# Two layers of a hybrid trunk: the first up phase by seven products of halves, the modulation sums in small steps across four stages

## The chip, the cores and the metric

The kernel runs on 1 core of a Trainium2 chip. The metric is device time in microseconds (us) of one execution. The core has TensorE (PE; its weight loads are shown as PEld), VectorE (DVE), ScalarE (ACT), GpSimd (POOL), and SyncE (SP), which here only issues DMAs from its queue, in order.

## The reference

1152 tokens (128 context, 1024 latent) of width 1024 go through two layers. Layer 0 has attention beside a short convolution, layer 1 a bidirectional recurrence with 8 heads (HGRN2); each is followed by a gated feed-forward block with a convolution. Everything is fp32.

```
def _modulation(cond, w_mod, b_mod):
    return jnp.split(jax.nn.silu(cond) @ w_mod + b_mod, 6, axis=-1)

def _conv_ffn(h, w_up, conv_w, w_down):
    u = _dwconv(h @ w_up, conv_w)          # w_up: 1024 x 5632, three taps along the tokens
    a, gt = jnp.split(u, 2, axis=-1)
    return (jax.nn.silu(gt) * a) @ w_down  # w_down: 2816 x 1024

...
    sh1_s, sc1_s, gt1_s, sh2_s, sc2_s, gt2_s = _modulation(cond_lat, w_mod[l], b_mod[l])
    xs = _layer_norm(ALPHA * xs + gt1_s * os_, ln1_g[l], ln1_b[l])
    fs = _conv_ffn(xs * (1 + sc2_s) + sh2_s, ffn_w_up[l], ffn_conv_w[l], ffn_w_down[l])
    xs = _layer_norm(ALPHA * xs + gt2_s * fs, ln2_g[l], ln2_b[l])
```

The modulation is a product of two condition vectors (context and latent) with a 1024 x 6144 matrix per layer. It is made in chunks of 512 columns, 12 per layer.

## The kernel before, in words

Every large fp32 product is made of three passes over rounded parts: `wsplit` (L103) cuts a weight into a high part (ScalarE, L108) and a low part (GpSimd, L109, or VectorE), the activations are kept as such a pair too, and `mm3` (L92) issues high x high, high x low and low x high. Its lines 93 to 95 stand for all such matmuls in the profile, so groups go by tiles. Weights come over a ring of two raw tiles and three split ones. From the end of attention on, the order of instructions on each engine is the order in which the program writes them (`manual_schedule`), and SP's DMAs keep that order too.

**Up phase of layer 0** (`ffn_up`, L941): 44 products (22 pairs of a gate and a value column block), each 3 x 8 x 3 = 72 matmuls of 388 columns into a PSUM tile of three banks ("psu"). `conv` (L969) follows one product behind, on ScalarE (L978) and VectorE (L979, 980, 984); the result goes to DRAM ("sd"). Beside it the phase makes 13 chunks of the modulation (`mod_pieces`, L154): 512 KB loads into two tiles, 16 VectorE operations (L170 for the first of each condition, L172), then eight 128 x 128 transposes on TensorE (L181) and two reductions on VectorE (L183). GpSimd makes the residual x*g + b of the nine token blocks (L265), which are stored. The first raw and split pieces of the down phase are made before the last products end.

**Up phase of layer 1** (`ffn_up_fast`, L1071): six direct products (n = 0 to 5), and meanwhile `sums` (L1125) makes differences of the halves of h on VectorE. Then 19 pairs go by seven products of halves: `operand` (L1203) makes the weight operand four products ahead (sums on VectorE, L1197 to 1201; high part on ScalarE, L1219; low part on GpSimd, L1220), `product` (L1230) issues 24 matmuls of 290 columns three-fold into a PSUM tile of two banks out of a ring of four ("psq"), and VectorE adds it into "u" (L1302 to 1313; L1313 is the last of a pair). The convolution of a pair is done during the next pair (L1243, L1248). At the seam into the seven products, line 1179 first splits the held third of the sums after the last convolution, then four operands are made (L1254). In the last pair the first two pieces of the down phase are loaded at the fifth product and split at the seventh (`split_s`, L1334), and the last modulation gate is stored at the fourth (`gate_store`, L193: 2 x 1024 pieces of 4 bytes).

**Down phase** (`ffn_down`, L1347): six groups of weight rows; in each, two column halves of nine token blocks. A unit (one half of one block) is 12 matmuls of 512 columns (6 in the first group) into one of six PSUM tiles ("psd"), copied by ScalarE in the first group (L1424) and added by VectorE in the others (L1426). In layer 1 alone the affine rows are loaded and scaled first (L1396, 1397, "gb"), and the residual is made unit by unit from the stored blocks (`residual_of`, L1400), with loads and stores over SP. The fifth group also multiplies by the gate on GpSimd (L1449) and adds on VectorE (L1453).

**Heads** (L1950 to 2033): for each of 8 heads 21 level steps (L1960) with projections for the next head between them.

Of the kernel before, what the change touches and what calls it, by code (L numbers as in the profile page):

```python
# [80 lines left out]
def build(tc, ins, outs, consts):  # L81
# [72 lines left out]
    def mod_pieces(l, f0, psp, tag):  # L154
# [30 lines left out]
        return load, compute, finish  # L185

# [754 lines left out]
    def ffn_up(l, hT, mod_list, xdst, steps, y, dw):  # L941

        with ExitStack() as st:
            fp = st.enter_context(tc.tile_pool(name=f"fp{l}", reuse_waits="tile", bufs=1))
            nonlocal accp, mbufs
            accp, mbufs = fp, 2
            pd = st.enter_context(tc.tile_pool(name=f"pdF{l}", reuse_waits="tile", bufs=2, space=PSUM))
            pu = st.enter_context(tc.tile_pool(name=f"puF{l}", reuse_waits="tile", bufs=2, space=PSUM))
            N = 2 * NF
            ws = {0: wpre.pop(0), 1: wpre.pop(0)}  # L950
            raws = {2: wraw(*up_cols(l, 2))}
            pss, cvs, pieces = {}, {}, []

            def bank():
                return pd.tile([P, 512], F32, tag="d", name="psl")

            def tmp():
                return fp.tile([P, 768], F32, tag="ht", bufs=2, name="ht")

            def products(n, order):  # L960
                if n not in pss:
                    pss[n] = pu.tile([P, 3, 512], F32, tag="u", name="psu")
                w, ps = ws[n], pss[n]
                for c, k in order:
                    a = c * OW
                    mm3(ps[:, c, :IW], (w[0][:, k, :], w[1][:, k, :]),
                        (hT[0].k(k, a, IW), hT[1].k(k, a, IW)), k == 0, k == KT - 1)

            def conv(n):  # L969
                ps, f = pss.pop(n), n // 2 if n % 2 else NF + n // 2  # L970
                t = fp.tile([P, SW], F32, tag="cv", bufs=4, name="cv")
                t3 = t.rearrange("p (a b) -> p a b", b=OW)
                cw = [fcw[:, l * 132 + q * 44 + f:l * 132 + q * 44 + f + 1] for q in range(3)]
                if n == N - 1:
                    last = fp.tile([P, 3, IW], F32, tag="last", name="last")
                    nc.scalar.activation(last, ps[:, :, :IW], AF.Copy)
                    ps = last
                nc.scalar.activation(t3, ps[:, :, 1:1 + OW], AF.Copy, scale=cw[1])  # L978
                nc.vector.scalar_tensor_tensor(t3, ps[:, :, 0:OW], cw[0], t3, op0=ALU.mult, op1=ALU.add)  # L979
                nc.vector.scalar_tensor_tensor(t3, ps[:, :, 2:2 + OW], cw[2], t3, op0=ALU.mult, op1=ALU.add)  # L980
                if n % 2 == 0:
                    nc.scalar.activation(t, t, AF.Silu)
                else:
                    nc.vector.tensor_tensor(t, t, cvs[n - 1], op=ALU.mult)
                cvs[n] = t

            def order(c):
                return [(c, k) for k in range(KT)]

            def store(n):  # L990
                if n > 0 and n % 2:
                    nc.sync.dma_start(sd[l][n // 2], cvs.pop(n))
                    cvs.pop(n - 1)

            def prepare(n):

                if n + 3 < N:
                    raws[n + 3] = wraw(*up_cols(l, n + 3))
                elif n + 3 - N < 2:
                    raws[n + 3] = wraw(*down_unit(l, n + 3 - N))  # L1000
                if n + 2 < N:
                    ws[n + 2] = wsplit(*raws.pop(n + 2))

            def mods_ahead():
                for a in range(2):
                    if not pieces and mod_list:
                        fs = mod_pieces(*mod_list.pop(0), pd, "d")
                        pieces.extend([(fs, b) for b in range(4)])
                    if pieces:
                        fs, b = pieces.pop(0)  # L1010
                        fs[0](b)
                        ready.append((fs, b))
            ready, ends = [], []
            gb = affine_rows(fp, l, 0)
            for n in range(N):

                while ends and ends[0][0] <= n - 2:
                    ends.pop(0)[1]()
                if n == 0:

                    for c in (2, 1, 0):
                        todo = steps.get(c - 1, [])
                        for x in range(2):
                            for kh in range(2):
                                products(x, order(c)[4 * kh:4 * kh + 4])
                                if todo:
                                    todo.pop(0)(bank, tmp)
                    nc.scalar.activation(gb, gb, AF.Copy, scale=ALPHA)
                elif n > 1:

                    products(n, order(2) + order(1) + order(0) if n < N - 1 else
                             [(c, 4 * kh + k) for kh in range(2) for c in (2, 1, 0) for k in range(4)])
                ws.pop(n)
                store(n - 2)
                if n == N - 1:

                    for u in range(2):
                        dws[u] = wsplit(*raws.pop(N + u))
                if n:
                    conv(n - 1)  # L1040
                prepare(n)
                for fs, b in ready:
                    fs[1](b)
                    if b == 3:
                        ends.append((n, fs[2]))
                ready.clear()
                if 2 <= n <= 18 and n % 2 == 0:
                    t = NT - n // 2
                    residual(y[t], gb, (nc.gpsimd, nc.gpsimd))
                if 4 <= n <= 20 and n % 2 == 0:  # L1050
                    t = NT + 1 - n // 2
                    nc.sync.dma_start(rows_of(xdst, t), y[t])
                if n >= 1:
                    mods_ahead()
                if n == 32:
                    gate_store(l, 5)
                if n == N - 4:
                    for a in range(2):
                        sraws.append(sraw(l, a, dw))
                if n == N - 1:  # L1060
                    for f in range(2):
                        split_s(l, f, dw)
                if l == 0 and n == 20:
                    gate_store(1, 2)
            conv(N - 1)
            store(N - 1)
            for _, f in ends:
                f()

    sraws = []  # L1070
    def ffn_up_fast(l, hT, steps, y):  # L1071
# [31 lines left out]
        def conv(n):  # L1103
            ps = pss.pop(n)
            t = fp.tile([P, 1160], F32, tag="t", bufs=3, name="cv")[:, :SW]
# [4 lines left out]
            nc.vector.scalar_tensor_tensor(t3, ps[:, :, 2:2 + OW], cw[2], t3, op0=ALU.mult, op1=ALU.add)  # L1110
            if n % 2 == 0:
# [3 lines left out]
            cvs[n] = t  # L1115
# [25 lines left out]
        for n in range(N0):  # L1141
            if n == 0:
                for c in (2, 1, 0):
                    todo = steps.get(c - 1, [])
                    for x in range(2):
                        for kh in range(2):
                            products(x, [(c, 4 * kh + k) for k in range(4)])
                            if todo:
                                todo.pop(0)(bank, tmp)
            elif n > 1:  # L1150
                products(n, [(c, k) for c in (2, 1, 0) for k in range(KT)])
            ws.pop(n)
            if n > 2 and n % 2:
                nc.sync.dma_start(sd[l][n // 2 - 1], cvs.pop(n - 2))
            if n:
                conv(n - 1)
            if n + 3 < N0 + 2:
                raws[n + 3] = wraw(*up_cols(l, n + 3))
            if n + 2 < N0:
                ws[n + 2] = wsplit(*raws.pop(n + 2))  # L1160
# [13 lines left out]
            if 1 <= n <= 4:  # L1174
                sums(n - 1)
# [997 lines left out]
```

## Time and profile before

| | us |
|---|---|
| median of 3 runs (3332.5 to 3335.68) | 3335.12 |
| the profiled execution: its own time | 3338.62 |
| its span | 3336.7 |
| TensorE busy | 3192.3 (96%) |
| VectorE busy | 2030.9 (61%) |
| GpSimd busy | 1262.8 (38%) |
| ScalarE busy | 1228.1 (37%) |

The stages: the start and attention to some 700 us, the up phase of layer 0 to 1280, its down phase to some 1590, the heads to some 2390, the up phase of layer 1 from 2492 to 3012, its down phase to the end. A timeline row gives start, duration, engine, line, operation, tiles, and in brackets how long the engine was idle before it and what ended that. Matmuls overlap, so a matmul's cost is the distance between starts.

### The profile page before, as it was taken

The numbers are of one execution on the slowest core, as the hardware profiler recorded it, in microseconds if no ns is written. First come the engines' busy times: TensorE is split into PE (matmuls) and PEld (weight loads), VectorE is DVE, ScalarE is ACT, GpSimd is POOL, SyncE is SP. The second block draws the span as 40 slices with busy tenths as digits, with TensorE's granted clock in tenths as the row PEclk, the third lists the DMA queues.
The fourth block names the chain that finished last, engine by engine and source line by source line (L and its number), as shares of the span: only waits on it lengthen the run. The fifth ranks groups of instructions, "written<-read, shape, count | busy, mean of one in ns | idle before, by whom it ended". The sixth has DMA issues, their size and how long they took to land. (4 is left out here: it accounts for less than half of the span.)

```text
span 3336.7 us, 46779 instructions
## 1 busy us (share of the span) xinstructions
PE 3192.3 (96%) x18671; PEld 2962.3 (89%) x18671; DVE 2030.9 (61%) x2912; ACT 1228.1 (37%) x2033; POOL 1262.8 (38%) x898
## 2 busy tenths in 40 slices
PE   7999999999999999998999999999999999997997
PEld 6989887789999998886999999998778999996886
DVE  5777888449997223355355455555557677773356
ACT  4412998232221224114433444433444333333112
POOL 6821333234431122242244443333424444442565
PEclk9999999999999999999999999999999999998999
DMA  7152000225564224231311111111322222225452
GB/s 216 34 145 77 1 1 32 80 79 174 160 167 132 64 74 135 87 126 44 115 62 40 49 42 55 55 49 44 114 95 73 73 73 73 74 78 145 155 175 82
DMA packets 264041, 295.87 MB, mean 89 GB/s; under 512 B 18467, under 2 KB 198895, under 8 KB 263824
## 3 DMA queue, kind: packets, MB, share of 16 engines
q1 hardware_dynamic: 263024, 291.25, 28.3%
q8 instruction: 147, 2.41, 0.3%
q0 software_dynamic: 800, 1.63, 0.2%
q14 instruction: 70, 0.57, 0.1%
HBM read 233.12 MB, written 59.72 MB: 88 GB/s over the span
## 5 line engine op out<-in xcount | busy, mean ns | idle before, releaser
L109 POOL TENSOR_TENSOR wlo<-wraw,whi 128x1024 fp32r<-128x1024 f32 x116 | 288.0, 2486 | 702.5 <-ACT whi L108 666.7
L93 PE MATMUL psd<-whi,s 128*128 128x512 f32 x720 | 286.1, 397 | 24.3 <-ACT y L1424 14.0
L94 PE MATMUL psd<-wlo,s 128*128 128x512 f32 x720 | 285.6, 397 | 0.0
L95 PE MATMUL psd<-whi,s 128*128 128x512 f32 x720 | 285.5, 397 | 0.0
L108 ACT ACTIVATE whi<-wraw 128x1024 fp32r<-128x1024 f32 x168 | 176.4, 1052 | 271.9 <-PE psd L95 82.3
L1696 POOL TENSOR_TENSOR X<-X,tot 128x384 f32<-128x384 f32 x144 | 183.4, 1274 | 212.6 <-PE pss L1690 142.9
L1426 DVE TENSOR_TENSOR y<-y,psd 128x512 f32<-128x512 f32 x144 | 98.8, 686 | 228.8 <-PE psd L95 228.6
L172 DVE SCALAR_TENSOR_TENSOR macc<-mraw,sil,macc 128x512 f32<-128x512 f32 x280 | 228.5, 881 | 14.6 <-DMA mraw<-in_w_mod_dram 14.5
L1696 DVE TENSOR_TENSOR X<-X,tot 128x384 f32<-128x384 f32 x144 | 90.3, 627 | 168.0 <-PE pss L1690 109.7
L93 PE MATMUL psu<-h,whi 128*128 128x388 f32 (+1 forms) x504 | 175.6, 349 | 14.0 <-DVE sc L600 7.6
L93 PEld LDWEIGHTS psd<-whi,s 128*128 128x128 f32 x720 | 136.6, 190 | 57.6 <-ACT y L1424 14.9
L93 PE MATMUL psu<-ra,whi 128*128 128x388 f32 x528 | 180.9, 343 | 2.9 <-DVE y L912 2.7
L95 PE MATMUL psu<-rb,wlo 128*128 128x388 f32 x528 | 179.9, 341 | 0.0
L94 PE MATMUL psu<-rb,whi 128*128 128x388 f32 x528 | 179.7, 340 | 0.0
L94 PE MATMUL psu<-ra,whi 128*128 128x388 f32 x528 | 179.6, 340 | 0.0
L93 PE MATMUL psu<-rb,whi 128*128 128x388 f32 x528 | 179.6, 340 | 0.0
L95 PE MATMUL psu<-ra,wlo 128*128 128x388 f32 x528 | 179.4, 340 | 0.0
L94 PE MATMUL psu<-h,whi 128*128 128x388 f32 (+1 forms) x504 | 174.7, 347 | 2.5 <-POOL h L389 2.4
L93 PE MATMUL psp<-s,whi 128*128 128x384 f32 x480 | 175.1, 365 | 0.0
L1690 PE MATMUL pss<-X,km 128*128 128x128 f32 x1008 | 152.4, 288 | 22.2 <-ACT km L1679 10.3
L95 PE MATMUL psu<-h,wlo 128*128 128x388 f32 (+1 forms) x504 | 173.2, 344 | 0.0
L93 PE MATMUL psp<-h,whi 128*128 128x384 f32 x480 | 173.1, 361 | 0.0
(413 smaller groups left out, 9645.9 us busy)
## 6 DMA issues: line engine op xcount, KB each, us to landing
wraw<-in_ffn_w_up_dram SPq DMA_DIRECT2D x88, 512.0 KB, 4.9
mraw<-in_w_mod_dram SPq DMA_DIRECT2D x80, 512.0 KB, 4.0
sraw<-sd SPq DMA_DIRECT2D x44, 578.0 KB, 4.4
wraw<-in_ffn_w_down_dram SPq DMA_DIRECT2D x44, 512.0 KB, 4.7
wraw<-in_hgrn_w_in_dram SPq DMA_DIRECT2D x40, 512.0 KB, 3.9
sd<-cv SPq DMA_DIRECT2D x25, 579.0 KB, 5.5
sd<-t SPq DMA_DIRECT2D x19, 578.0 KB, 2.9
wraw<-in_attn_w_in_dram SPq DMA_DIRECT2D x18, 512.0 KB, 4.0
```

The costliest lines, as they stand in the source:

```text
L93: mm(ps, l[0], r[0], start=start, stop=False)
L94: mm(ps, l[0], r[1], start=False, stop=False)
L95: mm(ps, l[1], r[0], start=False, stop=stop)
L108: nc.scalar.activation(hi[:, :n], raw[:, :n], AF.Copy)
L109: (eng or nc.gpsimd).tensor_tensor(lo[:, :n], raw[:, :n], r32(hi[:, :n]), op=ALU.subtract)
L172: nc.vector.scalar_tensor_tensor(acc[:, cond, :], r, sil[:, cond, k:k + 1], acc[:, cond, :], op0=ALU.mult, op1=ALU.add)
L1426: nc.vector.tensor_tensor(y[t][:, cols], y[t][:, cols], ps, op=ALU.add)
L1690: mm(ps[:, q3 * P:(q3 + 1) * P], km[:, q3 * P:(q3 + 1) * P], scan_ap(X, QAB, QAF, c0, P, hh), start=True, stop=True)
L1696: eng.tensor_tensor(x, x, t4[:, :, :, 1 - half].unsqueeze(3).to_broadcast([P, 2, nb, hh]), op=ALU.mult)
```

## The change

Layer 0's up phase is made by the function that layer 1 used, now called for both. The modulation chunks are made by a generator, `mod_steps`, one step at a time: one 256 KB load per step into a single tile, two VectorE operations per step, and at the end of a chunk eight matmuls against a column of ones. 3 chunks are made in layer 0's up phase and 2 in layer 1's (a step after every fourth product), 4 in the first down phase (ten steps per group, groups two to five), 4 in the heads (after every second level step). At the seam into the seven products, the first four operands are made before the last convolution but one, and the held sums are split between the sums and the end of the last convolution. In the last pair, the first pieces of the down phase are loaded at the third product and split at the sixth and seventh; the gate store moves to the thirteenth of the 19 pairs; the second down unit's split moves behind the convolution. The residual of layer 0 is made in its down phase as in layer 1. The convolution tile ring goes from 3 to 2; the gate store (1, 2) moves from layer 0's up phase to the fifth head; two temporary tiles of the first down phase's tail become halves of one tile.

```
+    def mod_steps(chunks, pool, bank):
+        for l, f0 in chunks:
...
+            acc = pool.tile([P, 2, 512], F32, tag="macc", name="macc")
+            for k in range(KT):
+                raw = pool.tile([P, 512], F32, tag="mraw", name="mraw")
+                nc.sync.dma_start(raw, wm[:, k, f0:f0 + 512])
+                yield True
+                for cond in range(2):
+                    if k == 0:
+                        nc.vector.tensor_scalar(acc[:, cond, :], raw, sil[:, cond, k:k + 1], None, op0=ALU.mult)
+                    else:
+                        nc.vector.scalar_tensor_tensor(acc[:, cond, :], raw, sil[:, cond, k:k + 1], acc[:, cond, :],
+                                                       op0=ALU.mult, op1=ALU.add)
+            yield True
+            ps = bank()
+            for cond in range(2):
+                for f in range(4):
+                    mm(ps[:, 4 * cond + f:4 * cond + f + 1], acc[:, cond, f * P:(f + 1) * P], ones, start=True,
+                       stop=True)
+            nc.vector.tensor_tensor(mods[:, l, :, c0:c0 + 4], ps[:, 0:8].rearrange("p (c f) -> p c f", f=4),
+                                    colA[:, l * 48 + c0:l * 48 + c0 + 4].unsqueeze(1).to_broadcast([P, 2, 4]),
+                                    op=ALU.add)
...
-    def ffn_up(l, hT, mod_list, xdst, steps, y, dw):
...
-    def ffn_up_fast(l, hT, steps, y):
+    def ffn_up(l, hT, mod_list, steps, y):
...
+            if n == N0 - 1:
+                pr[P0] = (raws.pop(N0 + 1)[0], raws.pop(N0)[0])
+                for o in range(4):
+                    operand(o)
             if n:
                 conv(n - 1)
...
-        conv(N0 - 1)
-        first.close()
-        for j in range(4):
-            put(3, j, held[:, j, :], nc.vector)
+        conv_sums(N0 - 1)
+        for j in range(4):
+            put(3, j, held[:, j, :], nc.gpsimd if j == 1 else nc.vector)
+        conv_end(N0 - 1)
+        first.close()
...
-                if last and q == 4:
+                if last and q == 2:
                     for f in range(2):
-                        raw = tp.tile([P, 4, HW], F32, tag=f"T1{f}", name="sraw").rearrange(
+                        raw = tp.tile([P, 4, HW], F32, tag=f"T2{f}", name="sraw").rearrange(
...
-                if last and q == 6:
-                    split_s(l, 0, None)
-                    split_s(l, 1, None)
+                if last and q > 4:
+                    split_s(l, q - 5, None)
...
                     keep(p - 1, old["t1"])
-                    if last:
+                    if p == P0 + 12:
                         gate_store(l, 5)
...
+                if o % 4 == 1 and p < NP - 1:
+                    next(mod, None)
...
-        dws[1] = wsplit(*raws.pop(1))
         t2 = conv_first(NP - 1, 1, us[1])
...
         conv_rest(NP - 1, 0, us[0], t1)
+        dws[1] = wsplit(*raws.pop(1))
...
-    def ffn_down(l, xsrc, dw, tail, pre):
+    def ffn_down(l, xsrc, mod_list, dw, tail, pre):
...
-            if l:
-                gb = affine_rows(lp, l, 0)
...
+            gb = affine_rows(lp, l, 0)
+            nc.scalar.activation(gb, gb, AF.Copy, scale=ALPHA)
+            xsum = xh[1]
...
+                        if gi and ((t + hf) % 2 or t == 0):
+                            next(mod, None)
...
+    ffn_up(0, rhsA, mod_todo[:3], steps, y)
...
+    y = ffn_down(0, xd[0], mod_todo[3:7], dw, tail0, {7: lambda: (first_raw(0), first_raw(1)), 4: lambda: first_split(0),
...
+    mod = mod_steps(mod_todo[7:11], rp, pst)
...
             hd.level(*e)
+            if n % 2 and h < 7:
+                next(mod, None)
...
+        if h == 4:
+            gate_store(1, 2)
...
+    ffn_up(1, hT, mod_todo[11:], steps, y)
```

## Rows read from the trace of the kernel before

**Rows 1.** Stretches: PE, PEld, DVE, ACT, POOL busy us; PEclk, DMA share, GB/s.

```profile
800.00:900.00 100.00, 100.00 (x575) 99.90 (x574) 95.85 (x94) 20.88 (x19) 43.31 (x16) 1.00 0.56 166
1700.00:2310.00 610.00, 600.05 (x3994) 593.84 (x3993) 317.53 (x642) 242.81 (x435) 247.54 (x188) 1.00 0.16 51
2700.00:2800.00 100.00, 100.00 (x749) 100.00 (x748) 76.92 (x70) 36.27 (x49) 46.08 (x31) 1.00 0.25 81
3000.00:3100.00 100.00, 77.28 (x351) 64.21 (x351) 36.48 (x33) 33.74 (x40) 28.84 (x12) 0.88 0.50 145
```

**Rows 2.** Timeline of ScalarE, line 978, in layer 0's up phase.

```profile
784.56 1.23 ACT L978 ACTIVATE cv<-psu,fcw 128x1158 f32<-128x1158 f32 x1 [4.89 <-PE psu L95]
...
797.34 1.23 ACT L978 ACTIVATE cv<-psu,fcw 128x1158 f32<-128x1158 f32 x1 [10.61 <-PE psu L95]
...
810.97 1.23 ACT L978 ACTIVATE cv<-psu,fcw 128x1158 f32<-128x1158 f32 x1 [4.89 <-PE psu L95]
```

**Rows 3.** Stretch of layer 1's up phase, instructions of tile psq alone.

```profile
2597.60:2994.00 396.40, 396.40 (x2960) 396.40 (x2959) 92.10 (x124) 11.72 (x18) 1.00 0.22 72
```

**Rows 4.** Timeline of TensorE in attention, fp32 matmuls of 64 columns.

```profile
413.24 1.00 PE L774 MATMUL ppf<-I,osb 128*128 128x64 f32 x8
414.05 0.71 PE L656 MATMUL S<-kst,qst 128*128 128x512 f32 x2
```

**Rows 5.** TensorE in layer 1, seam into the seven products; a wait.

```profile
2572.28 0.34 PE L95 MATMUL psu<-s,wlo 128*128 128x388 f32 x1
2577.60 0.61 PE L93 MATMUL psq<-h,whi 128*128 128x290 f32 x1 [4.99 <-ACT whi L1219]
...
2594.41 0.30 PE L93 MATMUL psq<-T,whi 128*128 128x290 f32 x1
...
PE psu L93 <- DVE cv L1110: 1.7, 3, 0.7
```

**Rows 6.** Timeline of TensorE entering the down phases, layer 0, then layer 1.

```profile
1280.23 0.40 PE L93 MATMUL psd<-whi,s 128*128 128x512 f32 x1
...
3022.99 0.77 PE L93 MATMUL psd<-whi,s 128*128 128x512 f32 x1 [10.29 <-ACT t L1243]
...
3046.36 0.80 PE L93 MATMUL psd<-whi,s 128*128 128x512 f32 x1 [12.43 <-ACT y L1424]
3046.95 0.63 PE L94 MATMUL psd<-wlo,s 128*128 128x512 f32 x1
```

**Rows 7.** Same seam on ACT, DVE, SP; then DMA issues, us to landing.

```profile
3018.19 1.17 ACT L1342 ACTIVATE s<-sraw 128x1156 fp32r<-128x1156 f32 x1 [14.13 <-DMA sraw<-sd]
...
3043.91 1.91 ACT L1397 ACTIVATE gb<-gb 128x2048 f32<-128x2048 f32 x1 [15.63 <-DMA gb<-in_ln_b_dram]
...
3022.09 0.75 DVE L1313 TENSOR_TENSOR u<-u,psq 128x580 f32<-128x580 f32 x1
...
3031.37 0.32 SPq L1252 DMA_DIRECT2D sd<-t  x1
...
gd<-mods SPq DMA_DIRECT2D x2, 4.0 KB, 11.3
...
x<-xd SPq DMA_DIRECT2D x3, 512.0 KB, 6.2
...
x<-xh SPq DMA_DIRECT2D x14, 256.0 KB, 2.9
...
mraw<-in_w_mod_dram SPq DMA_DIRECT2D x80, 512.0 KB, 4.0
```

**Rows 8.** Groups by line of VectorE, 800 to 1000.

```profile
L172 DVE SCALAR_TENSOR_TENSOR macc<-mraw,sil,macc 128x512 f32<-128x512 f32 x106 | 88.2, 900 | 0.4 <-DMA mraw<-in_w_mod_dram 0.4
L170 DVE TENSOR_SCALAR macc<-mraw,sil 128x512 f32<-128x512 f32 x14 | 32.1, 2330 | 0.0
```

**Rows 9.** Stretches of layer 1's down phase, an early and the fifth group.

```profile
3122.00:3172.00 50.00, 50.00 (x217) 40.42 (x217) 19.04 (x23) 8.71 (x8) 23.86 (x10) 1.00 0.51 165
3222.00:3272.00 50.00, 49.01 (x211) 39.04 (x210) 42.65 (x39) 6.59 (x6) 44.19 (x22) 1.00 0.46 160
```

More of the change, by code (lines that the diff above doesn't have):

```diff
@@ L185, in mod_pieces @@
         return load, compute, finish
+    ones = cst.tile([P, 1], F32, name="ones")
+    nc.vector.memset(ones, 1.0)
+    def mod_steps(chunks, pool, bank):
+        for l, f0 in chunks:
+            wm = ins["w_mod"][l].rearrange("(k p) f -> p k f", p=P)
+            c0 = f0 // P
+            acc = pool.tile([P, 2, 512], F32, tag="macc", name="macc")
[18 more added lines that the diff above has]
+                                    op=ALU.add)
     pending = []
@@ L939, in down_unit @@
         return w_dn[:, f0:f0 + 2, hf * 512:(hf + 1) * 512], 2, 512
-    def ffn_up(l, hT, mod_list, xdst, steps, y, dw):
[L943 to L1068, printed above, removed]
@@ L1139, in sums @@
             put(4, j, b21, nc.gpsimd)
[L1141 to L1160, printed above, removed]
[L1161 to L1182 removed]
         P0, NP = N0 // 2, NF
         NO = 7 * (NP - P0)
[L1185 removed]
+        wts, S, pr = {}, {}, {}
         def pair_raws(p):
@@ L1252, in keep @@
             nc.sync.dma_start(sd[l][p][:, :2 * HO].rearrange("p (a b) -> p a b", b=HO), t)
-        for o in range(4):
-            operand(o)
+        for n in range(N0):
+            if n == 0:
+                for c in (2, 1, 0):
+                    todo = steps.get(c - 1, [])
+                    for x in range(2):
+                        for kh in range(2):
+                            products(x, [(c, 4 * kh + k) for k in range(4)])
+                            if todo:
+                                todo.pop(0)(bank, tmp)
+            elif n > 1:
+                products(n, [(c, k) for c in (2, 1, 0) for k in range(KT)])
+            ws.pop(n)
+            if n > 2 and n % 2:
+                nc.sync.dma_start(sd[l][n // 2 - 1], cvs.pop(n - 2))
+            if n == N0 - 1:
+                pr[P0] = (raws.pop(N0 + 1)[0], raws.pop(N0)[0])
+                for o in range(4):
+                    operand(o)
+            if n:
+                conv(n - 1)
+            if n + 3 < N0 + 2:
+                raws[n + 3] = wraw(*up_cols(l, n + 3))
+            if n + 2 < N0:
+                ws[n + 2] = wsplit(*raws.pop(n + 2))
+            if n == 0:
+                for t in range(NT - 1, -1, -1):
+                    nc.sync.dma_start(rows_of(xd[l], t), y[t])
+                ypool["st"].close()
+            if n == 1:
+                fgs.close()
+                tps = ExitStack()
+                tp = tps.enter_context(tc.tile_pool(name=f"tp{l}", reuse_waits="tile", bufs=1, side="right"))
+                for m in (1, 2, 4):
+                    ts[m] = [tp.tile([P, 4, HW], F32R, tag=f"T{m}{q}", name=f"T{m}{q}") for q in range(2)]
+                ts[3] = [hT[q].halves[0][:, :, HW:2 * HW] for q in range(2)]
+                held = tp.tile([P, 4, HW], F32, tag="u", bufs=2, name="held")
+            if 1 <= n <= 4:
+                sums(n - 1)
+        conv_sums(N0 - 1)
[3 more added lines that the diff above has]
+        first.close()
+        pq = fs.enter_context(tc.tile_pool(name=f"pq{l}", reuse_waits="tile", bufs=4, space=PSUM))
         nc.sync.dma_start(sd[l][P0 - 1], cvs.pop(N0 - 1))
         old = None
+        mod = mod_steps(mod_list, fp, lambda: pq.tile([P, 2, 512], F32, tag="q", name="psq")[:, 0, :])
         for p in range(P0, NP):
@@ L1455, in ffn_down @@
                 nc.vector.tensor_tensor(a, a, b, op=ALU.add)
+            assert next(mod, None) is None
             su.close()
@@ L1522, in build @@
     prj.close()
+    mod_todo += [(1, f0) for f0 in range(512, 6144, 512)]
+    ffn_up(0, rhsA, mod_todo[:3], steps, y)
     dwx = ExitStack()
-    dw = dwx.enter_context(tc.tile_pool(name="dw", reuse_waits="tile", bufs=1))
-    ffn_up(0, rhsA, mod_todo + [(1, f0) for f0 in range(512, 6144, 512)], xd[0], steps, y, dw)
+    dw = dwx.enter_context(tc.tile_pool(name="dw0", reuse_waits="tile", bufs=1))
     w_in = ins["hgrn_w_in"][0]
```

66 lines of the change are left out of this document (29 added, 37 removed).

## The prediction

> **What bounds the kernel now.** First the busy time by stretches [rows 1]: TensorE is busy in 100 of 100 us of both up phases and in 600 of 610 us of the heads; only around 3000 to 3100, where layer 1's up phase hands over, it falls to 77 of 100. So TensorE's instructions set the time, and the few places where it stands still. Second, what one product costs. In layer 0 ScalarE's line 978 starts once per direct product, 12.78 us apart, or 13.63 where the eight transposes of a modulation chunk lie between [rows 2]. In layer 1 the matmuls of the seven-product path run at 396.4/2960 = 0.1339 us each [rows 3]. Third, the two seams of layer 1's up phase, one into the seven products and one into the down phase, since layer 0 gets both [rows 5 to 7]. About 0.2% (6.7 us) is what a measurement of this kernel can tell from no change; the chances below go by it.
>
> **The products.** A direct pair costs 2 x 12.78 = 25.56 us; a pair by seven products is 7 x 24 = 168 matmuls x 0.1339 = 22.50 us. 19 of the 22 pairs change: 19 x 3.06 = **-58.1 us**. That layer 0 reaches layer 1's rate is taken from rows 3: same shapes, same function.
>
> **The sums' small matmuls.** Layer 0's up phase loses the transposes of 13 chunks, 13.63 - 12.78 = 0.85 us each: **-11.0**. In their place each chunk gets eight fp32 matmuls with one moving column. TensorE is the bound in all four stages that get them (3, 4, 4 and 2 chunks), so all of it counts. No such matmul is in the trace. The nearest row is line 774: four fp32 matmuls of 64 columns, eight records, 0.81 us until the next instruction starts [rows 4], so 0.20 each. The transposes (0.85/8 = 0.11 each) are the lower end, twice line 774 the upper. I take 0.20: 8 x 0.20 x 13 = **+21.1**.
> The Trainium skill ("FP8 and Floating Point Precision", TensorE Precision Notes) says that a true fp32 matmul makes four passes through the array; the eight records for four matmuls show two. By four passes of 0.1 us the term would be 42 us, not 21.
>
> **The sums' VectorE work.** Per chunk there are two first and fourteen further operations, as before. The further ones take 0.90 us on the mean of a stretch of the direct up phase, the first ones 2.33 there [rows 8]. In the up phases a step of two operations comes every four products (12.9 us) and adds some 1.8 us to a VectorE that is busy 77%, so 91%; in 800 to 900 it was at 96% and TensorE still at 100 of 100 [rows 1]. The cover is the four PSUM tiles, one product each; without it every late microsecond of VectorE would be one of TensorE. I cost it at nothing. In the heads VectorE is at 52% and TensorE is idle 10 us in 610 [rows 1]; 36 steps are added there: **+2** (0 to 15). In the down phase I take **+5** (0 to 19) for the last group, where VectorE is already busy 42.65 of 50 us [rows 9] and gets 6 steps; why a larger loss is possible there is the first rival.
>
> **The seam into the seven products.** In layer 1 the last direct matmul starts at 2572.28 and the fourth product at 2594.41 [rows 5]: 22.1 us for three products of 3.21, so 12.3 lost. It begins with the wait for the first operand (line 1219, 4.99 us). The change issues four operands one product earlier, under 12.8 us of matmuls. What is late next is the last third of the sums of h, which the third product needs 6.4 us in: the convolution's one ScalarE copy (1.2, rows 2), two VectorE passes over 1158 columns and one over 580, at most 2.0, 2.0 and 1.0 by line 172's 0.90 for 512 columns [rows 8] (an estimate). That is 6.2, just in time. I leave 1 us of stall (0 to 12.3): layer 1 **-11.3**, layer 0 **+1.0**. Layer 0's direct products now share VectorE with those sums as layer 1's do, where TensorE waits three times, 1.7 us in all [rows 5]: **+1.7**.
>
> **The seam into the down phase.** Layer 0 has none today: its first down matmul, at 1280.23, has no idle time before it. Layer 1 stands 10.29 us (from 3012.7), does six units, and stands 12.43 [rows 6]. The first stand goes back to the loads of the first pieces. They are queued behind the gate store, which takes 11.3 us to land [rows 7]; they reach ScalarE at 3018.19, and VectorE's last sum waits behind those splits until 3022.09 [rows 7]. The change moves the gate store six pairs ahead and the loads two products ahead, so they have 10 us and no store before them: that stand goes. What is late next is the second one: ScalarE waits 15.63 us for the affine rows, with the evacuations queued behind [rows 7]. Those loads are issued behind the phase's last store (3031.37) and land when some 3.8 MB have passed, which I leave as long as it is. The last store comes 9.3 us after VectorE's last sum starts (four passes and a product of the convolution lie between); that sum moves from 3022.09 to 3012.6, right after the last matmul. So all of it shifts by 9.5, and TensorE resumes at 3036.9: layer 1 **-9.5**. Layer 0 gets the same seam: 24.2 us from the last product to the resume, less six units of 1.4 (six matmuls each, 217 in 50 us in rows 9), plus 2.4 because a dozen matmuls after a stand run slower (0.63 where 0.40 is usual, rows 6; the granted clock is 0.88 in that stretch, rows 1), which costs 0.2 each: **+18.2** where it had nothing.
>
> **The rest.** The residual (18 GpSimd passes and 18 transfers) moves from layer 0's up phase to its down phase. Layer 1's down phase has it already: GpSimd is busy 23.86 of 50 us, the DMA half, and TensorE 50.00 [rows 9]; nothing. On SP each load of the sums waits until VectorE has freed the one tile, and weight loads queue behind it: in the up phases they have five products of slack, in the heads two projections; nothing. One convolution tile less means a wait on a store that has four products to land; nothing. The gate store in the heads holds up loads by its 11 us, less than those two projections; nothing.
>
> **Sum.** -58.1 - 11.0 + 21.1 + 2 + 5 - 11.3 + 1.0 + 1.7 - 9.5 + 18.2 = -40.9. The profiled execution's own time is 3338.6, so 3297.7; the median of the runs lies 3.5 below it: **3294 us**.
>
> **Rivals.** (1) *The loads of the sums in the first down phase; the slower case.* With one tile a step is a loop: landing, two operations, next issue, so about the landing plus 2.0 us. VectorE works in order, so the evacuations stand behind a late load. Ten steps come in a group of 49.9 us, 5.0 us each, 36 in all, and six PSUM tiles of 2.77 us cover 16.6 us once. Pieces of 256 KB landed in 2.9 us in the last group of layer 1, the residual's of 512 KB in 6.2 [rows 7]. At 2.9 a step fits. At 4.0 (the old 512 KB loads, rows 7) TensorE loses 36 x 1.0 - 16.6 = 19, less the 5 already counted: 3308. At 6.2 it loses 36 x 3.2 - 16.6 = 99: 3388. From a landing of 4.7 us on the change is slower than before. For it speaks that SP's order holds each load behind waits on GpSimd; against it the 2.9, the nearest row in size and stage. Chances .18 for the milder form, .06 for slower. (2) *The first pieces still come late*, because they queue behind two weight loads: both layers keep the first stand, 9.5 each: 3313; .10. (3) *The small matmuls cost twice as much*: +21, 3315; .05; the record count of line 774 speaks against it. The four passes of the Trainium skill's page named above would be this case. (4) *The affine rows land sooner*, in both layers by 5: 3284; .06. That the change doesn't do what it says is no case of its own: layer 1 already runs the path.
>
> **How the numbers follow.** Forecast .55, the others as given. Faster by over 0.2%: .91; within it .03 (landings near 4.7); slower .06. The range 3274 to 3320 holds the forecast and rivals 2, 3, 4 and the milder 1, with one seam better or worse by some 10 us.
>
> **What would show it.** Right: 100 of 100 us and some 748 matmuls per 100 us in layer 0's up phase, which ends near 1219; no wait on line 1219 at either seam; one stand of about 15 us in each layer's first down group, ended by the affine rows; VectorE waiting under 2 us a time for the sums' loads. Wrong: TensorE waiting on VectorE's line 1426 within the first down phase; a split still waiting for its load at an up phase's end; a heads' stretch longer by over 10 us.

## The result, and the profile after

The changed kernel takes 3349.78 us (median of 4 runs, 3349.18 to 3354.56), the kernel before in the same comparison 3333.81: a ratio of 1.0047, interval 1.0034 to 1.006. It is slower by 0.5%, where 3294 was forecast. The profiled execution took 3349.69 (span 3347.9), 11.1 more than that of before.

By stages, each from the first matmul into its own PSUM tile to the first into the next stage's (layer 1 to its last matmul; what lies between changes by under 1 us a time):

| stage | before | after | forecast | measured |
|---|---|---|---|---|
| layer 0 up (from 702) | 578.0 | 526.3 | -61.5 | -51.7 |
| layer 0 down, to its last group | 228.5 | 292.2 | +29.7 | **+63.7** |
| heads | 781.8 | 789.5 | +8.5 | +7.7 |
| layer 1 up and down | 828.6 | 821.5 | -17.6 | -7.1 |

So the products gave what they should, and the loss sits in the first down phase (34 us worse than forecast) and in the seams into the seven products (some 9 each). Stretches of the changed kernel, to be held against [rows 1, 9] (columns as there):

```profile
800.00:900.00 100.00, 100.00 (x748) 100.00 (x747) 84.45 (x84) 34.28 (x46) 46.60 (x30) 1.00 0.33 104
1230.00:1280.00 50.00, 34.48 (x140) 27.42 (x139) 15.68 (x12) 24.14 (x32) 12.39 (x5) 0.83 0.50 167
1280.00:1521.00 241.00, 215.36 (x893) 174.96 (x892) 149.28 (x170) 31.94 (x30) 114.00 (x51) 0.91 0.50 165
1700.00:2310.00 610.00, 598.82 (x3980) 591.13 (x3979) 357.75 (x674) 241.15 (x432) 245.77 (x186) 1.00 0.20 60
```

Up phase and heads are as full as before. The third line is the new thing: in groups two to five of the first down phase TensorE is idle for 25.6 of 241 us and at a clock of 0.91. Who it waited for, by the waits of TensorE (us in all, times, longest):

```profile
PE psd L93 <- ACT y L1337: 31.9, 2, 16.3
PE psl L210 <- DVE macc L204: 24.8, 5, 10.9
PE psq L93 <- DVE cv L1010: 15.8, 2, 7.9
```

And the same waits in TensorE's timeline, in order of time, with the small matmuls of one undisturbed chunk (916.14) ahead of them as a measure:

```profile
916.14 1.84 PE L210 MATMUL psq<-ones,macc 128*128 128x1 f32 x16
917.85 0.38 PE L93 MATMUL psq<-T,whi 128*128 128x290 f32 x1
...
795.23 0.58 PE L93 MATMUL psq<-T,whi 128*128 128x290 f32 x1 [7.87 <-DVE cv L1010]
...
1252.47 0.80 PE L93 MATMUL psd<-whi,s 128*128 128x512 f32 x1 [15.52 <-ACT y L1337]
...
1327.13 1.86 PE L210 MATMUL psl<-ones,macc 128*128 128x1 f32 x8 [5.78 <-DVE macc L204]
1329.88 1.86 PE L210 MATMUL psl<-ones,macc 128*128 128x1 f32 x8 [0.88 <-DVE macc L204]
...
1382.31 3.08 PE L210 MATMUL psl<-ones,macc 128*128 128x1 f32 x16 [4.29 <-DVE macc L204]
...
1434.96 3.54 PE L210 MATMUL psl<-ones,macc 128*128 128x1 f32 x16 [2.94 <-DVE macc L204]
...
1496.73 3.55 PE L210 MATMUL psl<-ones,macc 128*128 128x1 f32 x16 [10.88 <-DVE macc L204]
...
3058.84 0.80 PE L93 MATMUL psd<-whi,s 128*128 128x512 f32 x1 [16.34 <-ACT y L1337]
```

TensorE stands at each of the four chunk ends, since the eight matmuls that finish a chunk need VectorE's accumulators and TensorE works in order. A stand also costs what follows it: from start to start the chunk at 916.14 takes 1.71 us, those behind a stand 2.9 to 3.6. The granted clock, 1.00 (2.4 GHz) on the ten us ahead of the first and the last of these stands, is between its two levels, 2.4 and 1.2 GHz, on the mean of the ten us behind them (stretch, TensorE busy, granted clock, DMA share, GB/s):

```profile
1310.00:1320.00 10.00, 10.00 (x45) 1.00 0.68 212
1329.00:1339.00 10.00, 9.12 (x33) 0.70 0.53 184
...
1475.00:1485.00 10.00, 10.00 (x44) 1.00 0.42 144
1497.00:1507.00 10.00, 10.00 (x35) 0.56 0.61 191
```

The +63.7 is then 15.5 for the affine rows, 24.8 at the chunk ends, 13.4 for the small matmuls there (6.8 at 1.71 a chunk), and 10.0 that remains. Matmul by matmul it is the large ones: less the waits, the distances between their starts add up to 11.7 us more than before, 1.7 to 2.8 behind each of the five stands and next to nothing elsewhere (before, TensorE's waits were 1.6).

Why VectorE is late at a chunk's end, by its timeline, GpSimd's and SP's:

```profile
1301.21 5.66 DVE L204 SCALAR_TENSOR_TENSOR macc<-mraw,sil,macc 128x512 f32<-128x512 f32 x2 [4.02 <-DMA mraw<-in_w_mod_dram]
1306.79 0.67 DVE L1339 TENSOR_TENSOR y<-y,psd 128x512 f32<-128x512 f32 x1
...
1313.88 1.41 DVE L204 SCALAR_TENSOR_TENSOR macc<-mraw,sil,macc 128x512 f32<-128x512 f32 x2 [0.24 <-DMA mraw<-in_w_mod_dram]
...
1321.50 1.41 DVE L204 SCALAR_TENSOR_TENSOR macc<-mraw,sil,macc 128x512 f32<-128x512 f32 x2 [3.73 <-DMA mraw<-in_w_mod_dram]
...
1455.17 1.41 DVE L204 SCALAR_TENSOR_TENSOR macc<-mraw,sil,macc 128x512 f32<-128x512 f32 x2 [1.86 <-DMA mraw<-in_w_mod_dram]
...
1495.83 1.41 DVE L204 SCALAR_TENSOR_TENSOR macc<-mraw,sil,macc 128x512 f32<-128x512 f32 x2 [1.62 <-DMA mraw<-in_w_mod_dram]
...
1301.10 2.41 POOL L1318 TENSOR_TENSOR x<-x,gb 128x1024 f32<-128x1024 f32 x1
1303.46 2.86 POOL L109 TENSOR_TENSOR wlo<-wraw,whi 128x1024 fp32r<-128x1024 f32 x1
...
1315.32 0.33 SPq L198 DMA_DIRECT2D mraw<-in_w_mod_dram  x1
```

The loop of the one tile can be followed (SP issues the next load once VectorE has freed the tile): the pair at 1313.88 ends at 1315.29, SP issues the next load at 1315.32, VectorE waits until it is there at 1321.50. From the first to the seventh of these pairs the fourth chunk takes 40.7 us (1455.17 to 1495.83), 6.8 a step; the other three, measured alike, take 5.9, 5.5 and 5.6. A step has 5.0. Over the 24 steps counted so, the two operations take 2.2 us of the 5.9 on the mean, and 3.8 pass from their end to the next pair's start. Over 1250 to 1500 two groups of VectorE, the sums' operations and the additions of a unit (busy us, mean ns, idle before), and below them the landing of the loads (count, size, median us):

```profile
L204 DVE SCALAR_TENSOR_TENSOR macc<-mraw,sil,macc 128x512 f32<-128x512 f32 x56 | 60.1, 1114 | 52.5 <-DMA mraw<-in_w_mod_dram 52.5
L1339 DVE TENSOR_TENSOR y<-y,psd 128x512 f32<-128x512 f32 x65 | 43.8, 682 | 42.2 <-PE psd L95 42.0
```

```profile
mraw<-in_w_mod_dram SPq DMA_DIRECT2D x32, 256.0 KB, 3.0
```

The median load lands in 3.0 us, as forecast (2.9, [rows 7]), and VectorE waits 52.5 us for the loads all the same: some come late, as the one from 1315.32 to 1321.50. The seam into the seven products, on VectorE and GpSimd:

```profile
779.09 1.93 DVE L1063 TENSOR_TENSOR S<-wraw 128x512 f32<-128x512 f32 x1
...
784.49 1.78 DVE L1067 TENSOR_TENSOR S<-wraw,S 128x512 f32<-128x512 f32 x1
786.97 1.42 DVE L1009 SCALAR_TENSOR_TENSOR cv<-psu,fcw,cv 128x1158 f32<-128x1158 f32 x1 [0.69 <-ACT cv L1008]
...
792.20 1.42 DVE L1009 SCALAR_TENSOR_TENSOR cv<-psu,fcw,cv 128x1158 f32<-128x1158 f32 x1 [2.35 <-ACT cv L1008]
793.66 1.42 DVE L1010 SCALAR_TENSOR_TENSOR cv<-psu,fcw,cv 128x1158 f32<-128x1158 f32 x1
...
776.58 5.74 POOL L1030 TENSOR_TENSOR T<-b,T 128x580 fp32r<-128x580 f32 x3 [7.61 <-ACT T L1029]
```

The four weight sums of the operands (7.2 us, 1.8 each beside GpSimd's passes) run ahead of both remaining convolutions. The second of these, which frees PSUM for the second product, has its ScalarE copy (line 1008) only behind the first one's end, and ends at 795.08.

### The profile page after: what moved, and what is told of

It reads as the page before. It is cut to its first block, busy times and chain, and to the rows that moved or that the text cites. A ratio compares the mean times of both kernels' runs of the same rounds, so it can differ in the third digit from the quotient of the medians.

```text
span 3347.9 us, 48705 instructions
## 1 busy us (share of the span) xinstructions
PE 3161.8 (94%) x19231; PEld 2927.0 (87%) x19231; DVE 2230.9 (67%) x3117; ACT 1290.1 (39%) x2162; POOL 1416.1 (42%) x1007
## 5 line engine op out<-in xcount | busy, mean ns | idle before, releaser
L1086 POOL TENSOR_TENSOR wlo<-S,whi 128x512 fp32r<-128x512 f32 x152 | 243.9, 1618 | 253.9 <-ACT whi L1085 253.8
L109 POOL TENSOR_TENSOR wlo<-wraw,whi 128x1024 fp32r<-128x1024 f32 x78 | 195.6, 2510 | 248.0 <-ACT whi L108 237.1
L93 PE MATMUL psq<-T,whi 128*128 128x290 f32 x912 | 272.2, 298 | 15.8 <-DVE cv L1010 15.8
L95 PE MATMUL psq<-T,wlo 128*128 128x290 f32 x912 | 272.4, 299 | 0.0
L94 PE MATMUL psq<-T,whi 128*128 128x290 f32 x912 | 272.0, 298 | 0.0
L1114 DVE SCALAR_TENSOR_TENSOR t<-u,fcw,t 128x1156 f32<-128x1156 f32 x152 | 259.1, 1722 | 13.5 <-ACT t L1109 10.8
L108 ACT ACTIVATE whi<-wraw 128x1024 fp32r<-128x1024 f32 x130 | 136.6, 1053 | 323.6 <-DMA wraw<-in_ffn_w_down_dram 151.1
L1086 POOL TENSOR_TENSOR wlo<-wraw,whi 128x512 fp32r<-128x512 f32 x114 | 182.3, 1600 | 172.8 <-ACT whi L1085 157.1
L1085 ACT ACTIVATE whi<-S 128x512 fp32r<-128x512 f32 x152 | 93.4, 628 | 335.8 <-DVE S L1064 247.5
L204 DVE SCALAR_TENSOR_TENSOR macc<-mraw,sil,macc 128x512 f32<-128x512 f32 x182 | 185.0, 1056 | 53.8 <-DMA mraw<-in_w_mod_dram 53.8
L93 PE MATMUL psu<-h,whi 128*128 128x388 f32 (+1 forms) x504 | 176.1, 350 | 13.7 <-DVE sc L629 6.5
L93 PEld LDWEIGHTS psq<-T,whi 128*128 128x128 f32 x912 | 173.8, 191 | 16.2 <-ACT whi L1085 16.2
L1612 PE MATMUL pss<-X,km 128*128 128x128 f32 x1008 | 152.3, 288 | 23.4 <-POOL X L1618 10.4
## 6 DMA issues: line engine op xcount, KB each, us to landing
sraw<-sd SPq DMA_DIRECT2D x44, 578.0 KB, 4.6
sd<-t SPq DMA_DIRECT2D x38, 578.0 KB, 3.0
```

Of the source, the lines that this page charges most:

```text
L93: mm(ps, l[0], r[0], start=start, stop=False)
L94: mm(ps, l[0], r[1], start=False, stop=False)
L95: mm(ps, l[1], r[0], start=False, stop=stop)
L108: nc.scalar.activation(hi[:, :n], raw[:, :n], AF.Copy)
L109: (eng or nc.gpsimd).tensor_tensor(lo[:, :n], raw[:, :n], r32(hi[:, :n]), op=ALU.subtract)
L204: nc.vector.scalar_tensor_tensor(acc[:, cond, :], raw, sil[:, cond, k:k + 1], acc[:, cond, :], op0=ALU.mult, op1=ALU.add)
```

## The experiments

Each is one edit of the changed kernel (line numbers are its own, 3349.8 its median); the kernel before took 3331.7 to 3334.4 beside them.

**Without the loads of the first down phase** (e1).

```
-                raw = pool.tile([P, 512], F32, tag="mraw", name="mraw")
-                nc.sync.dma_start(raw, wm[:, k, f0:f0 + 512])
+                raw = gb[:, 0, :512]          # first down phase only
```

> The changed kernel, but the modulation sums of the first down phase read a row tile that is in SBUF already, so the 32 loads of 256 KB are left out there (those four chunks of the modulation come out as other numbers); all VectorE operations, the small matmuls and the residual stay. Theory A (the loop of one tile makes VectorE late, and TensorE, which works in order, stands at the four places where it needs a finished accumulator): TensorE's waits on line 204 in the first down phase fall from 24.8 us to under 5, the half clock behind them goes too, the stage falls from 292 to 250 to 260 us, total 3349.8 to 3310 to 3320. Rival B (GpSimd's residual passes stretch the two VectorE operations from 1.4 to 4 to 5.7 us, and that alone makes VectorE late): more than 15 us of those waits stay, total 3338 or above.

Measured: 3314.95 us. Waits of TensorE:

```profile
PE psl L213 <- DVE macc L207: 3.3, 2, 2.8
```

The same VectorE operations beside the same GpSimd passes: without the loads the stage takes 260.1 instead of 292.2. Theory A stands, as far as the loads go.

**Without the residual in layer 0's down phase**, whole (e2), its passes alone (e9), its transfers alone (e10).

```
-            stream = [... (residual_of(t, gb),) * 6]
+            stream = [... (residual_of(t, gb),) * 6] if l else []
```

> The changed kernel, but layer 0's down phase leaves the residual out (9 loads and 9 stores of 512 KB and 18 GpSimd passes; the output lacks the scale and shift of that residual); the sums and their loads stay. Theory A (loop of one tile): the waits on line 204 stay above 15 us, total 3338 to 3350. Rival B (the residual's GpSimd passes or its transfers make the sums late): the waits fall under 5 us, total 3310 to 3322.

Measured: 3325.01, waits on line 204 10.0 us in two: between the two theories, neither of which holds as written. The residual has a share in it.

```
                 for a, op in enumerate((ALU.mult, ALU.add)):
-                    nc.gpsimd.tensor_tensor(x, x, gb[:, a, :], op=op)
+                    if l: nc.gpsimd.tensor_tensor(x, x, gb[:, a, :], op=op)       # e9
+                    nc.gpsimd.tensor_tensor(x, x if l else gb[:, 1 - a, :], gb[:, a, :], op=op)  # e10, no DMAs
```

> The changed kernel, but in layer 0's down phase the residual's 18 GpSimd passes are left out; its loads and stores of 512 KB stay (the output lacks that scale and shift). e2_nores, without both, had 10.0 us of waits on line 204 and 3325. Theory P (the passes, which stretch VectorE's operations and hold the stores behind them in SP's order, are what the residual does to the sums): near e2_nores, waits 6 to 14 us, total 3321 to 3331. Theory X (its transfers, ahead of the sums' loads in SP's queue and beside them in the DMA engines): near the changed kernel, waits 20 us or more, total 3342 to 3352.

> The counterpart of e9_xfer: in layer 0's down phase the 18 GpSimd passes stay, on rows that are in SBUF, and the residual's 9 loads and 9 stores are left out (the output has the residual without scale and shift). Theory P (the passes count): near the changed kernel, waits on line 204 20 us or more, total 3342 to 3352. Theory X (the transfers count): near e2_nores, waits 6 to 14 us, total 3321 to 3331.

Measured: 3329.25 without the passes, 3347.40 without the transfers. TensorE's wait and VectorE's group (1250 to 1500), e9 first:

```profile
PE psl L210 <- DVE macc L204: 12.8, 2, 11.5
```

```profile
L204 DVE SCALAR_TENSOR_TENSOR macc<-mraw,sil,macc 128x512 f32<-128x512 f32 x56 | 48.2, 902 | 44.2 <-DMA mraw<-in_w_mod_dram 44.2
```

And e10:

```profile
PE psl L210 <- DVE macc L204: 23.4, 5, 10.2
```

```profile
L204 DVE SCALAR_TENSOR_TENSOR macc<-mraw,sil,macc 128x512 f32<-128x512 f32 x56 | 66.8, 1233 | 41.0 <-DMA mraw<-in_w_mod_dram 41.0
```

Theory P: of the residual it is the passes. Beside them one operation takes 1.1 or 1.2 us in place of 0.90, and a step has two; its 9 MB of transfers do 2 to 4 us.

**Three tiles for the loads** (e13). Two of them lie in a weight buffer that the phase needs only for its unit 20; loads go out two steps ahead.

```
-                raw = pool.tile([P, 512], F32, tag="mraw", name="mraw")
-                nc.sync.dma_start(raw, wm[:, k, f0:f0 + 512])
+                load(k + 2)                   # into tile k % 3, load(0) and load(1) ahead
                 yield True
```

> The changed kernel with three tiles for the sums' pieces in the first down phase and each load issued two steps ahead (two of the tiles lie in the third weight buffer of that phase, whose units are dealt over five buffers); all loads, operations, places and passes stay. Theory A (the one tile is the cause: each load waits for VectorE to free it, and lands too late): TensorE's waits on line 204 fall from 24.8 us to under 6, near the 3.3 of e1_noload, total 3349.8 to 3314 to 3325. Rival S (the loads are late whatever the number of tiles, since SP issues them in order behind other waits, or VectorE is simply too slow beside GpSimd): 12 us or more stay, total 3332 or above.

Measured: 3319.38. Waits of TensorE:

```profile
PE psl L218 <- DVE macc L212: 3.6, 2, 2.8
```

VectorE no longer waits for these loads at all (52.5 us before; 1250 to 1500):

```profile
L212 DVE SCALAR_TENSOR_TENSOR macc<-mraw,sil,macc 128x512 f32<-128x512 f32 x56 | 75.0, 1377 | 0.0
```

All loads, passes and operations are there, and the operations are even longer than in the changed kernel (1377 ns for 1114), so it is the one tile, at this spacing, that turns late loads and long operations into stands of TensorE. The edit also deals the phase's weights over other buffers, which was not tried by itself.

**Places of the steps.** At every second unit (e11), and the small matmuls of a chunk one step later (e6).

```
-                        if gi and ((t + hf) % 2 or t == 0):
+                        if gi and (9 * hf + 8 - t) % 2 == 0:
```

> The changed kernel with the 36 steps of the first down phase at every second unit (5.5 us apart) where they stood 2.8 or 5.5 us apart; nothing is left out. Theory D (what piles up is the neighbouring steps, two per group, which leave 2.8 us for a loop of 5 or more): waits on line 204 at 10 us or less, total 3325 to 3335. Theory M (the mean spacing of 5 to 5.5 us is itself about as long as the loop): waits 15 us or more, total 3338 to 3350.

Measured: 3344.59, waits 22.2 us in four. Theory M: 5.5 us is itself too short.

```
-            ps = bank() ... mm(...) ... nc.vector.tensor_tensor(mods...)
+            late = finish                      # called before the next chunk's first operation
```

> The changed kernel with the eight small matmuls of each chunk one step later in the order (just before the next chunk's first operation on the same accumulators), in all stages; loads, VectorE operations and their places stay. Theory (what costs is that TensorE, in order, meets the finishing matmuls at a moment when VectorE is behind): the waits on line 204 lose some 5 us at each of the four places, 24.8 to 10 or less, total 3349.8 to 3325 to 3335. Rival (VectorE's lag itself sets TensorE's pace through the six PSUM tiles): what is gained there comes back as waits of TensorE on line 1339, total 3345 to 3352.

Measured: 3337.55. The chunk ends in TensorE's timeline:

```profile
1328.39 1.05 PE L200 MATMUL psl<-ones,macc 128*128 128x1 f32 x8 [1.47 <-DVE macc L223]
...
1376.43 1.95 PE L200 MATMUL psl<-ones,macc 128*128 128x1 f32 x16 [0.76 <-DVE macc L223]
...
1424.30 1.84 PE L200 MATMUL psl<-ones,macc 128*128 128x1 f32 x16
...
1482.27 3.54 PE L200 MATMUL psl<-ones,macc 128*128 128x1 f32 x16 [17.05 <-DVE macc L223]
```

The first three stands shrink to 1.47, 0.76 and nothing, and the small matmuls behind them are faster, but the last grows from 10.88 to 17.05: lag that is not waited for stays. Neither text had that. The first down phase is 13.7 us shorter, 5.4 of it in TensorE's waits, 4.6 in the small matmuls and 3.7 in the large ones behind the stands.

**Two chunks to the heads** (e5), the steps of the other two every third unit.

```
-    y = ffn_down(0, xd[0], mod_todo[3:7], dw, tail0, ...
+    y = ffn_down(0, xd[0], mod_todo[3:5], dw, tail0, ...
-    mod = mod_steps(mod_todo[7:11], rp, pst)
+    mod = mod_steps(mod_todo[5:11], rp, pst)
-                        if gi and ((t + hf) % 2 or t == 0):
+                        if gi and (9 * hf + t + 1) % 3 == 0:
```

> The changed kernel with two of the four chunks of the first down phase moved to the heads (six there), so that 18 steps stand every third unit (8.3 us apart) where 36 stood 2.8 to 5.5 us apart; nothing is left out. Theory (a step needs some 5 to 8 us for its one tile to be freed, loaded and used, so steps closer than that pile up until a chunk's end): TensorE's waits on line 204 fall from 24.8 us to under 4 in the first down phase and stay near 0 in the heads; the down phase loses 35 to 40 us, the heads gain two chunks of 1.7 us and little else, total 3349.8 to 3312 to 3320. Rival (VectorE is too slow there with GpSimd beside it, whatever the spacing): two chunk ends are left with 5 us or more each, total 3330 or above.

Measured: 3312.75. The down phase falls to 247.9, with no wait on line 204 left; the heads grow by 9.3 for two chunks, where the first four cost 7.7 and the expectation had 3.4.

**The affine rows scaled behind the first group** (e3), and the first group's splits in its second half as well (e7).

```
-            nc.scalar.activation(gb, gb, AF.Copy, scale=ALPHA)
...
             for gi, grp in enumerate(FGROUPS[:-1]):
+                if gi == 1:
+                    nc.scalar.activation(gb, gb, AF.Copy, scale=ALPHA)
...
-                        if t in (7, 5, 4, 2) and nf < ... and (t > 3 or gi == 0):
+                        if t in (7, 5, 4, 2) and nf < ... and (t > 3 or gi == 0) and (gi or hf):   # e7
```

> The changed kernel, but ScalarE scales the affine rows behind the evacuations of the first group instead of before them, in both down phases. Theory: the two stands of TensorE (15.5 and 16.3 us, on ScalarE's line 1337) go, with some 2 us of half clock behind each; total 3349.8 to 3310 to 3320. Rival: the stand passes to the next thing that is late (the splits of the first weights, or the first residual), and less than 12 us of the 32 comes back: 3338 or above.

Measured: 3338.03. What ScalarE waits for then, and TensorE's stand:

```profile
1244.90 1.17 ACT L1256 ACTIVATE s<-sraw 128x1156 fp32r<-128x1156 f32 x1 [10.75 <-DMA sraw<-sd]
...
1246.61 0.79 PE L93 MATMUL psd<-whi,s 128*128 128x512 f32 x1 [7.68 <-ACT y L1338]
```

The rival: half of the stand passes to the next late load in ScalarE's order. At the chunk ends TensorE now waits 28.7 us where it had waited 24.8.

> As e3_gblate (affine rows scaled behind the first group), and the four splits of the first group moved from its first half to its second, so that no evacuation of the first half stands behind a load. Theory (in e3_gblate the stand is set by the load of the first split piece, which SP issues behind the phase's last store): the two stands of 7.7 and 8.7 us shrink to under 4 each, total 3338.0 to 3325 to 3332. Rival (the second group needs those four splits, so the stand only moves to its start): as e3_gblate, 3335 to 3341.

Measured: 3328.17. No wait on line 1338 is left, only some 3 us in layer 0 and 4 in layer 1 on the splits.

**Convolutions between the operands** (e4) at the seam into the seven products.

```
-                for o in range(4):
-                    operand(o)
-            if n:
-                conv(n - 1)
+                operand(0); conv_sums(n - 1); operand(1)
+                conv_sums(n); conv_end(n - 1); operand(2); operand(3)
```

> The changed kernel, but at the last direct product of both up phases the two remaining convolutions are put between the weight sums (operand 0, first convolution, operand 1, second convolution, operands 2 and 3) instead of behind all four operands. Theory: TensorE's wait for the second product (7.9 us in each layer, on line 1010) falls to 4 us or less in each, total 3349.8 to 3340 to 3344. Rival: the operands 2 and 3 then come as much later as the convolutions came earlier, the stand moves to the third or fourth product, total 3347 to 3352.

Measured: 3341.53. In layer 0:

```profile
787.77 0.38 PE L93 MATMUL psq<-T,whi 128*128 128x290 f32 x1 [3.33 <-DVE cv L1010]
...
794.01 0.40 PE L94 MATMUL psq<-ra,whi 128*128 128x290 f32 x1 [2.24 <-POOL ra L1030]
...
781.46 0.68 DVE L1063 TENSOR_TENSOR S<-wraw 128x512 f32<-128x512 f32 x1
```

The theory, with a small new wait at the third product, the one that the forecast had feared. The weight sums, which here find GpSimd idle (780.21 to 783.67), take 0.68 us each. From the first product to the fourth 6.1 us are still lost in layer 0 and 6.3 in layer 1, so the order of the convolutions explains some 8 of the 20 us lost in both; the rest was not taken apart.

**Together.** e8: e4, e5 and e7.

> The changed kernel with e4_seam, e5_heads and e7_defer together; nothing is left out. Theory: the gains add, as they lie in different places: 8 from e4_seam, 32 to 37 from e5_heads, 12 to 22 from e3_gblate and e7_defer: 3349.8 to 3283 to 3298, faster than the kernel before by 36 to 51. Rival (a stand that goes at one seam comes back behind it): 3305 or above.

Measured: 3280.21, ratio to the kernel before 0.9836 (0.982 to 0.9852): 69.6 below the changed kernel, where the three alone sum to 8.3 + 37.0 + 21.6 = 66.9. The first down phase:

```profile
1223.00:1458.00 235.00, 231.34 (x1005) 186.70 (x1005) 158.00 (x147) 57.58 (x62) 127.89 (x55) 0.99 0.56 186
```

Three variants of it: one chunk to the heads instead of two (e12); all four in the down phase through three tiles (e14); the same with the steps at every second unit (e15).

> As e8_all, but only one chunk goes to the heads: three stay in the first down phase, with steps 5.5 and 8.3 us apart by turns (6.9 on the mean); nothing is left out. If a step needs under 7 us on the mean the third chunk costs its 1.7 us in the down phase and takes some 4.6 us from the heads (what each of the two cost there, 9.2 us together): 3280.2 to 3275 to 3279. If it needs more, the waits on line 204 come back with 3 us or more: 3281 to 3292.

Measured: 3293.56, with 9.3 us of waits on line 204: 6.9 us a step is still too little for one tile, a little more costly than the expectation allowed.

> As e8_all, but with all four chunks in the first down phase, fed through three tiles as in e13_tiles, and four in the heads as in the changed kernel; nothing is left out. By theory A the two chunks cost 1.7 us each in the down phase, and the heads get back what they cost there (9.2 us in e5_heads): 3280.2 to 3272 to 3280. By rival S the waits come back: 3290 or above.

Measured: 3285.09, between the two. The heads get their 7.5 back (789.0), but the down phase takes 248.2 where e8 has 235.0. Of the 13.2 us, the small matmuls are 4.4, the waits 3.9, and the large matmuls behind the stands 4.9 (granted clock 0.83 from 1395 to 1405 and 0.70 from 1452 to 1462).

> As e14_alltiles, with the 36 steps at every second unit. If neighbouring steps still matter with three tiles: 2 to 6 us less than e14_alltiles. If not: within 2 us of it.

Measured: 3288.20, 3.1 us more than e14, which neither text had. The first down phase itself takes 248.6 where e14 has 248.2, so with three tiles the even spacing gains nothing there.

## Why the prediction was wrong

**Right.** The products: 2903 matmuls in 388.0 us, 0.1337 each as in [rows 3]:

```profile
812.00:1200.00 388.00, 388.00 (x2903) 388.00 (x2903) 88.69 (x122) 11.17 (x17) 1.00 0.28 89
```

The small matmuls: 1.71/8 = 0.21 each at the full clock, forecast 0.20. By the four passes of the Trainium skill ("FP8 and Floating Point Precision", TensorE Precision Notes) the term was estimated at 42 us; the row shows 16 records for eight matmuls, two each, and at the full clock the lower price. The heads: +7.7, forecast +8.5. The seam into the down phase: from the end of the products to the resume 25.1 us in layer 0 (1227.40 to 1252.47) and 24.9 in layer 1 (3033.95 to 3058.84), forecast 24.2, ended by the affine rows, as said:

```profile
1250.02 1.91 ACT L1309 ACTIVATE gb<-gb 128x2048 f32<-128x2048 f32 x1 [16.89 <-DMA gb<-in_ln_b_dram]
```

**Wrong, 34 us: the sums in the first down phase.** The step that failed is the term for the sums' VectorE work there, +5 (0 to 19). With the small matmuls' 6.5 it had 11.5 us for the four chunks; the waits at their ends (24.8), the small matmuls (13.4) and the slower large ones behind those stands (9) came to some 47. Rival 1 named the loop of the one tile, and priced it too low in three ways. First, the step: the landing plus 2.0 us, 4.9 for 5.0, with the change slower only from a landing of 4.7. The median landing is 3.0, and still a step takes 5.5 to 6.8, 5.9 on the mean: 2.2 for the two operations, which wait for GpSimd's passes (0.90 to 1.11 us each, e9 and e10), and 3.8 until the next pair starts, because the median hides the late loads (6.2 us from 1315.32 to 1321.50). By the rival's own sum that is 36 x 0.9 - 16.6 = 16 us. Second, the cover: six PSUM tiles save TensorE from waiting for a free tile, but four times in the phase it must itself wait for the accumulator, so what VectorE was late by then was a stand. The forecast's sign for this case, TensorE waiting on the additions (line 1426, now 1339), did not come; the stands came in front of the small matmuls. Third, the lower clock behind the stands, priced at the seam but not here: 6.6 us at the small matmuls and some 9 at the large ones. e1 and e13 take the loop away, with 34.8 and 30.4 us back.

**Wrong, 18 us: the seam into the seven products.** Forecast -11.3 and +1.0. From the first product to the fourth it takes 19.6 us in layer 0 (783.98 to 803.53) and 20.0 in layer 1, for three products of 3.21: 9.9 and 10.4 lost, where layer 1 had lost 12.3 [rows 5]. The step that failed is the stall left at that seam, 1 us: it said that with the operands earlier the last third of the sums of h is late next, for the third product. It asked what makes an operand, and not what frees the PSUM tile of the second product: the last convolution, which now stands behind the four weight sums on VectorE, whose 7.2 us were put at nothing. e4 shows it for some 8 us of the 18; the rest stays open.

## What to carry to other kernels

A load into a single tile is a loop: landing, the reader's wait in its own queue, its operations at their duration beside other engines, the next issue. Hold that sum against the spacing of the steps, and if it is near, give it a second tile or more room before anything else. PSUM tiles cover lateness only as long as the engine that fills them does not itself wait for the late one: look for every place where it does, and add the lower clock behind each stand. At a seam, ask for each instruction what makes its input and also what frees its output.

## What was not expected of the hardware

VectorE's operation on two SBUF inputs takes 0.7 us alone (1.41 for a pair), and the pair at 1301.21 took 5.66: it started just after one GpSimd pass (1301.10) and ended just after the next (1303.46 to 1306.32). The addition of a PSUM tile (line 1339), with one SBUF input, keeps 0.68 on the mean of the same stretch. The Trainium skill ("SBUF — State Buffer", Who interferes with whom) says that a VectorE instruction with two SBUF inputs contends with a GpSimd instruction that reads SBUF, and calls the port pair that they share an exclusive lock; the trace agrees, and the forecast had not drawn on it. The weight sums at the seam, 1.8 us beside GpSimd and 0.68 without in e4, show the same. The clock was the other surprise: a stand of 2.94 us was followed by small matmuls at twice their time.
